# A two-layer hybrid trunk on one core: the scheduler orders the instructions by a simulated timeline

## The chip, the cores and the metric

The kernel runs on one core of one Trainium2 chip. A time is the device time of one execution of the whole program, in microseconds (us); less is better. Engines are written as in the profile: PE is TensorE (matmuls; PEld are its weight loads), DVE is VectorE, ACT is ScalarE, POOL is GpSimd, SP is SyncE, which issues nearly all DMAs. "L421" is line 421 of the kernel file.

## The reference

The reference is the trunk of a diffusion model: two layers over 256 latent tokens and 256 context tokens with 1024 channels, all in float32. Per layer:

```python
h = modulate(rmsnorm(x, norm1_g[l]), sh1, sc1)          # shifts and scales are silu(c) @ w_ada + b_ada
p = h @ w_in[l]                                         # GLU halves, q, k, v, gates
y_conv = conv_branch(p[..., :GLU_END], ...)             # GLU, depthwise conv of 31 taps, LayerNorm, silu, @ w_conv_out
y_attn = merge_heads(neighbourhood_attention(q, k, v, k_c, v_c, rpb)) @ w_na_out[l]
x = x + g1 * gated_merge(p[..., QKV_END:], y_conv, y_attn, w_out[l])
h2 = modulate(rmsnorm(x, norm2_g[l]), sh2, sc2)
x = x + g2 * conv_ffn(h2, w_up[l], ffn_dw[l], ffn_dw_b[l], w_down[l])   # FFN 2816, conv of width 3
```

Eight heads of 64 channels attend to a window of a 64-wide grid and to all context tokens. The context stream goes through the same weights, but its second layer needs only keys and values. A final RMSNorm ends it.

## The kernel before

Everything lies transposed: channels on the 128 partitions, tokens (256 latent, then 256 context) along the free axis, so a matmul has a 128x128 block of weights as stationary operand and 512 tokens (256 in the last layer) as moving one. float32 products are made of three fp32r products (L176 to L179): the weight and the activation are each split into a high and a low part.

```python
def mm3(ps, w, xh, xl, start, stop):
    pe.matmul(ps, w[0], xh, start=start, stop=False)     # L177
    pe.matmul(ps, w[0], xl, start=False, stop=False)     # L178
    pe.matmul(ps, w[1], xh, start=False, stop=stop)      # L179
```

Weights come in units of 128x1024 (512 KB) that SP fetches into one of four "raw" buffers (L155); ACT rounds a unit to its high part (`whi`, L158) and DVE subtracts to get the low part (`wlo`, L159). PSUM has four banks for `main`, two for `sc` (head scores), one for `pt` (transposes) and one for `po`.

The program is written as one row of weight groups. Other work is cut into steps by generators, and `slot()`, called within and behind each group, advances every generator that is open by one step. These side rows are:

- Attention of a layer. `product` (L417 to L421) makes the scores of two heads, each on its own 64 rows of the array, for 128 queries; `ctx` products are the same with 256 columns. `scores` (L437 to L445) adds the bias (DVE, L437), takes the maximum (DVE, L439), the exponential (ACT, L442), the reciprocal of the sum (DVE, L444) and multiplies (ACT, L445). `turn` transposes the probabilities on PE (L475, L480), ACT copies them (L476, L481), and `values` (L494) multiplies with V, each head on its own 64 columns of the array; L500 and L501 split the output. Queries and keys get their rotary part and their split on DVE at L740 to L747.

```python
for n, (a, b) in enumerate(((0, 0), (0, 1), (1, 0))):
    for o, r in zip(out, HALF):
        pe.matmul(o, q[r, a, c], k[r, b, d], start=n == 0, stop=n == 2)      # L421
```

- The depthwise convolution of 31 taps per channel tile, one DVE instruction per tap (L566, L568), at a fixed number of taps a step; the LayerNorm behind it.
- The adaLN products of later parts: on PE at the start and in the middle (L200, four groups of 32 columns; ACT copies the rows at L217, PE transposes them at L224), on DVE as dot products (L260) otherwise.
- The norms. The residual is added at L877, squares are summed (ACT L307, DVE L311), PE sums them over the channels with a column of ones (L325, tile `pt`), DVE scales (`red`, L333), POOL takes the power -1/2 (`rs`, L335), PE spreads it over the partitions (L340, tile `po`), and `modulated` makes h: DVE L354, ACT's high part L355, DVE's low part L356. In the FFN of layer 1 and behind the output projection of layer 0 this lies beside matmuls of other tiles.

No engine order is written out by hand, save a few edges (`tc.issue_after`). The functions above emit instructions in program order; the tile framework's scheduler then builds, from their dependences, one queue for each engine, with the semaphores between them, and hands out the slots of the pools in that order. [...]

## Time and profile before

| | |
|---|---|
| time, three runs | 1138.9, 1140.42, 1144.16 us (median 1140.42) |
| the profiled execution | time 1141.42 us, span 1139.6 us, mean granted PE clock 0.996 |
| instructions in the span | 17741 |
| HBM read | 187.57 MB, 166 GB/s over the span |
| stages (by the timeline) | start to 62 us; attention of layer 0, 75 to 205; output side and norm 2, 205 to 402; FFN, 402 to 725; layer 1's attention, 800 to 880; its FFN from 955; tail from 1130 |

The span runs from the first to the last instruction; the profiled execution's time has 1.8 us around it. A row of the timeline gives start, duration, engine, line, operation, what is written from what, shape and count (instructions of one kind in a row are joined); a square bracket gives idle time before it and who ended it. Matmuls overlap, so the step from one start to the next tells more than a duration.

### The profile page before, as it was taken

To read this page: it belongs to the slowest core of one execution; us is meant where nothing else is said; L and a number is where in the kernel's file an instruction comes from. 1 tells how busy PE (TensorE), PEld (TensorE's weight loads), DVE (VectorE), ACT (ScalarE), POOL (GpSimd) and SP (SyncE) were. 2 spreads that over 40 slices of the span, in tenths; PEclk is the share of its full clock that TensorE was granted. 3 is DMA by queue.
4 is the path that set the end of the run, shared out by engine and by line. 5 is a ranking of instruction groups with operands and counts; after the bars stand their busy time and mean duration, and the time that the engine had idled before them with its cause. 6 is when DMAs were issued, how large, how long until landed. Compare 5 with 4: busy or idle time off the path is not lost.

```text
span 1139.6 us, 17741 instructions
## 1 busy us (share of the span) xinstructions
PE 1123.0 (99%) x6854; PEld 962.8 (84%) x6854; DVE 916.4 (80%) x1620; ACT 567.9 (50%) x930; POOL 17.3 (2%) x25
## 2 busy tenths in 40 slices
PE   9999999999999999999999999999999999999997
PEld 7677777787779978888888888988889999999996
DVE  4689999937598698888888555789997889988773
ACT  4357667424334444343434222544678577666541
POOL 0000000000000000000000000010000000000000
PEclk9999999999999999999999999999999999999999
DMA  8832312644645255554557666565434574666781
GB/s 323 304 101 72 102 49 91 208 143 133 198 150 168 74 154 161 163 170 137 177 147 236 210 195 193 183 194 156 134 114 153 162 236 148 215 186 185 224 258 56
DMA packets 54949, 189.78 MB, mean 167 GB/s; under 512 B 6352, under 2 KB 6352, under 8 KB 54864
## 3 DMA queue, kind: packets, MB, share of 16 engines
q1 hardware_dynamic: 54576, 188.60, 52.8%
q8 instruction: 54, 0.88, 0.3%
q14 instruction: 31, 0.25, 0.1%
q10 hardware_dynamic: 288, 0.04, 0.0%
HBM read 187.57 MB, written 1.05 MB: 166 GB/s over the span
## 4 chain that ended last, share of the span: by engine, by line
PE 73%; issue 17%; DVE 5%; DMA 2%; ACT 2%; POOL 0%; POOLq 0%; DVEq 0%; ACTq 0%; SPq 0%
PE main L177 20%; PE main L179 20%; PE main L178 20%; PE main L621 4%; PE po L494 2%; PE sc L421 2%; DMA raw<-in_wall 2%; DVE wlo L159 1%; PE sc L127 1%; ACT whi L158 1%; PE pt L475 1%; DVE t L260 1%; PE po L200 1%; PE sc L179 1%; PE main L475 1%
## 5 line engine op out<-in xcount | busy, mean ns | idle before, releaser
L177 PE MATMUL main<-h,whi 128*128 128x256 f32 (+1 forms) x1328 | 449.1, 338 | 1.1 <-ACT h L871 0.5
L179 PE MATMUL main<-h,wlo 128*128 128x256 f32 (+1 forms) x1328 | 444.1, 335 | 0.9 <-DVE wlo L159 0.9
L178 PE MATMUL main<-h,whi 128*128 128x256 f32 (+1 forms) x1328 | 443.0, 334 | 1.0 <-DVE h L872 1.0
L158 ACT CAST whi<-raw 128x1024 fp32r<-128x1024 f32 (+1 forms) x244 | 252.3, 1038 | 285.4 <-PE main L178 136.5
L159 DVE TENSOR_TENSOR wlo<-raw,whi 128x1024 fp32r<-128x1024 f32 (+1 forms) x244 | 293.0, 1207 | 115.5 <-ACT whi L158 110.8
L177 PEld LDWEIGHTS main<-h,whi 128*128 128x128 f32 x1328 | 249.6, 188 | 33.4 <-issue 5.7
L179 PEld LDWEIGHTS main<-h,wlo 128*128 128x128 f32 x1328 | 249.9, 188 | 29.7 <-DVE wlo L159 1.7
L178 PEld LDWEIGHTS main<-h,whi 128*128 128x128 f32 x1328 | 250.1, 188 | 29.2 <-DVE h L872 1.5
L568 DVE SCALAR_TENSOR_TENSOR cb<-u,par,cb 128x512 f32<-128x512 f32 (+1 forms) x240 | 140.1, 616 | 1.2
L260 DVE CUSTOM_DVE_ANT_0 t<-raw,sb,par 128x1024 bf16<-128x1024 f32 x100 | 126.8, 1278 | 2.3 <-DMA raw<-in_wada 2.3
L177 PE MATMUL main<-fh,whi 128*128 128x256 f32 (+1 forms) x386 | 123.0, 319 | 0.0
L178 PE MATMUL main<-fl,whi 128*128 128x256 f32 (+1 forms) x386 | 122.9, 318 | 0.0
L179 PE MATMUL main<-fh,wlo 128*128 128x256 f32 (+1 forms) x386 | 122.9, 318 | 0.0
L940 ACT ACTIVATE t<-main,par 128x512 f32<-128x512 f32 (+1 forms) x82 | 50.8, 669 | 62.6 <-PE main L179 62.5
L178 PEld LDWEIGHTS main<-fl,whi 128*128 128x128 f32 x386 | 72.7, 188 | 5.6
L179 PEld LDWEIGHTS main<-fh,wlo 128*128 128x128 f32 x386 | 72.7, 188 | 5.6
L177 PEld LDWEIGHTS main<-fh,whi 128*128 128x128 f32 x386 | 72.7, 188 | 5.5
L941 DVE SCALAR_TENSOR_TENSOR t<-main,par,t 128x510 f32<-128x510 f32 (+1 forms) x82 | 47.7, 615 | 13.6 <-ACT t L940 13.3
L944 DVE SCALAR_TENSOR_TENSOR t<-main,par,t 128x510 f32<-128x510 f32 (+1 forms) x82 | 46.8, 610 | 0.0
L355 ACT ACTIVATE h<-t,mod 128x256 fp32r<-128x256 f32 x56 | 25.0, 501 | 34.7 <-DVE t L354 34.7
L966 ACT CAST fh<-t 128x256 fp32r<-128x256 f32 (+1 forms) x43 | 22.0, 511 | 37.9 <-DVE t L956 37.3
L621 PE MATMUL main<-whi,h 128*128 128x512 f32 x128 | 40.6, 402 | 0.0
(178 smaller groups left out, 1194.0 us busy)
## 6 DMA issues: line engine op xcount, KB each, us to landing
raw<-in_wall SPq DMA_DIRECT2D x239, 512.0 KB, 4.2
raw<-in_wada SPq DMA_DIRECT2D x88, 512.0 KB, 4.3
bias<-in_bias_t SPq DMA_DIRECT2D x16, 256.0 KB, 3.9
row<-in_wada SPq DMA_DIRECT2D x8, 512.0 KB, 4.9
sb<-in_crow SPq DMA_DIRECT2D x5, 512.0 KB, 5.2
x<-in_xt SPq DMA_DIRECT2D x8, 256.0 KB, 4.2
raw<-in_wall SPq DMA_DIRECT2D x8, 256.0 KB, 7.3
out<-t SPq DMA_DIRECT2D x4, 256.0 KB, 2.6
```

The lines of the kernel that those rows point to most:

```text
L158: act.copy(hi[:, c], r[:, c])
L159: dve.tensor_tensor(lo[:, c], r[:, c], hi[:, c].bitcast(F32), ALU.subtract)
L177: pe.matmul(ps, w[0], xh, start=start, stop=False)
L178: pe.matmul(ps, w[0], xl, start=False, stop=False)
L179: pe.matmul(ps, w[1], xh, start=False, stop=stop)
L260: dve.tensor_tensor_reduce(tmp().bitcast(BF16), r, v, 1.0, pr(l, BADA + n, 1), ALU.mult, ALU.add, mods[l][:, n, s : s + 1])
L355: high = act.activation(hi[:, c], y[:, c], AF.Identity, bias=b)
L568: dve.scalar_tensor_tensor(cb[j], src, w, cb[j], ALU.mult, ALU.add)
L621: pe.matmul(pv[t], h1[n == 1][k][:, c], w[n == 2][:, b], start=k + n == 0, stop=k == KD - 1 and n == 2)
L940: act.activation(c, pv_, AF.Identity, bias=pr(l, FDB + t, 1), scale=w[1])
L941: dve.scalar_tensor_tensor(c[:, :, 1:], pv_[:, :, : S - 1], w[0], c[:, :, 1:], ALU.mult, ALU.add)
L944: dve.scalar_tensor_tensor(c[:, :, : S - 1], pv_[:, :, 1:], w[2], c[:, :, : S - 1], ALU.mult, ALU.add)
```

## The change

One argument of the context in which the program is built. Without it the scheduler takes, for each engine, what is ready from a list; with it the scheduler plays the program on a simulated timeline of the engines and orders every engine's queue by that.

```diff
@@ -1168,7 +1168,7 @@
     out = nc.dram_tensor("out_0", (KD // 2, P, 2 * S), F32, kind="ExternalOutput").ap()
-    with tile.TileContext(nc) as tc:
+    with tile.TileContext(nc, schedule_with_timeline_sim=True) as tc:
         trunk(tc, *args, out)
```

The instructions are the same, but for the loads of ACT's function table, of which there are 15 in place of 17. Each engine's queue has another order, and 654 of 2105 tiles another slot of their pool. At three places that the prediction speaks of, the listings of the two programs read as follows (line, operation, tile written <- tiles read, shape; x3 is three in a row).

PE in layer 0's attention, scores of the first head pair for the second half of the queries (`sc_862` and `sc_863` are the two heads'). Before:

```order
L178 MATMUL main_827<-h_205,whi_829 128x512
L179 MATMUL main_827<-h_197,wlo_830 128x512
L421 MATMUL sc_862<-qk_761,qk_715 128x512
L421 MATMUL sc_863<-qk_761,qk_715 128x512
L421 MATMUL sc_862<-qk_761,qk_715 128x512
L421 MATMUL sc_863<-qk_761,qk_715 128x512
L421 MATMUL sc_862<-qk_761,qk_715 128x512
L421 MATMUL sc_863<-qk_761,qk_715 128x512
L177 MATMUL main_895<-h_190,whi_897 128x512
L178 MATMUL main_895<-h_198,whi_897 128x512
```

and with the change:

```order
L178 MATMUL main_895<-h_205,whi_897 128x512
L179 MATMUL main_895<-h_197,wlo_898 128x512
L421 MATMUL sc_862<-qk_761,qk_715 128x512 x3
L421 MATMUL sc_863<-qk_761,qk_715 128x512 x3
L475 MATMUL pt_944<-ident,pp_812 128x128 x4
L475 MATMUL main_951<-ident,pp_821 128x128 x4
L177 MATMUL main_989<-h_190,whi_991 128x512
L178 MATMUL main_989<-h_198,whi_991 128x512
L179 MATMUL main_989<-h_190,wlo_992 128x512
```

The six matmuls of the two heads no longer alternate, three of one head come before three of the other, and transposes (L475) follow where a weight group did.

DVE in layer 0's attention, softmax of the last head pair (`sc_1725` and `sc_1726` are scores, `mx` maxima, `ri` reciprocals, `cb` the convolution's sums). Before:

```order
L568 SCALAR_TENSOR_TENSOR cb_2_208<-u_0_219,par,cb_2_208 128x512
L566 TENSOR_SCALAR cb_3_209<-u_1_220,par 128x512
L437 TENSOR_TENSOR sc_1725<-sc_1725,bias_1525 128x256
L437 TENSOR_TENSOR sc_1726<-sc_1726,bias_1525 128x256
L439 TENSOR_REDUCE mx_1748<-sc_1725 128x1
L439 TENSOR_REDUCE mx_1757<-sc_1726 128x1
L568 SCALAR_TENSOR_TENSOR cb_2_208<-u_0_219,par,cb_2_208 128x512
L444 RECIPROCAL ri_1753<-sm_1751 128x1
L159 TENSOR_TENSOR wlo_1982<-raw_1980,whi_1981 128x1024
L444 RECIPROCAL ri_1762<-sm_1760 128x1
```

and with the change:

```order
L501 TENSOR_TENSOR ol_2_216<-po_1670,oh_2_212 128x512
L437 TENSOR_TENSOR sc_1725<-sc_1725,bias_1525 128x256
L437 TENSOR_TENSOR sc_1726<-sc_1726,bias_1525 128x256
L568 SCALAR_TENSOR_TENSOR cb_2_208<-u_0_219,par,cb_2_208 128x512
L568 SCALAR_TENSOR_TENSOR cb_3_209<-u_1_220,par,cb_3_209 128x512
L439 TENSOR_REDUCE mx_1748<-sc_1725 128x1
L439 TENSOR_REDUCE mx_1757<-sc_1726 128x1
L568 SCALAR_TENSOR_TENSOR cb_3_209<-u_1_220,par,cb_3_209 128x512
L159 TENSOR_TENSOR wlo_2114<-raw_2112,whi_2113 128x1024
L568 SCALAR_TENSOR_TENSOR cb_3_209<-u_1_220,par,cb_3_209 128x512
L444 RECIPROCAL ri_1753<-sm_1751 128x1
L444 RECIPROCAL ri_1762<-sm_1760 128x1
```

The taps of `cb_2` up to there and many of `cb_3` now stand ahead of these rows; of the ones shown, four taps of `cb_2` and `cb_3` and a split (`wlo_2114`, which stood further behind) lie within the softmax.

PE at the norm behind layer 0's output projection (`pt_3325` the sums of the latent stream, `po_3361` the spread rsqrt, `h_2548` on the first tile of the normalised h's high part). Before, with the twelve rows between as a line of dots:

```order
L178 MATMUL main_3312<-h_2562,whi_3155 128x256
L325 MATMUL pt_3325<-one,ss_2983 128x1 x2
L179 MATMUL main_3312<-h_2554,wlo_3156 128x256
L177 MATMUL main_3312<-h_2555,whi_3155 128x256
L178 MATMUL main_3312<-h_2563,whi_3155 128x256
...
L179 MATMUL main_3348<-h_2551,wlo_3162 128x256
L340 MATMUL po_3361<-ident,rs_3330 128x128 x2
L177 MATMUL main_3348<-h_2552,whi_3161 128x256
```

and with the change:

```order
L177 MATMUL main_3450<-h_2555,whi_3173 128x256
L178 MATMUL main_3450<-h_2563,whi_3173 128x256
L179 MATMUL main_3450<-h_2555,wlo_3174 128x256
L325 MATMUL pt_3325<-one,ss_2983 128x1 x2
L340 MATMUL po_3361<-ident,rs_3330 128x128 x2
L177 MATMUL sc_3508<-h_2548,whi_3485 128x256
L177 MATMUL sc_3509<-h_2548,whi_3491 128x256
L177 MATMUL main_3510<-h_2548,whi_3497 128x256
```

The sums and the transposes have moved behind the last group of the output projection (`main_3450`), and the first matmuls that read the normalised h (`h_2548`, on `sc_3508` and others) come right behind them.

## The prediction

> **What bounds the kernel now.** I read the page's engine row first, then the list of waits, then busy time by stretch, then the timeline at the places that the change touches.
>
> From the page of before:
>
> ```profile
> PE 1123.0 (99%) x6854; PEld 962.8 (84%) x6854; DVE 916.4 (80%) x1620; ACT 567.9 (50%) x930; POOL 17.3 (2%) x25
> ```
>
> TensorE is busy for 1123.0 of 1139.6 us. The kernel is a row of matmuls, and a new order can win only the gaps in that row. The list of waits of PE (engine, line, who is waited for: us in total, times, longest) says how much that is:
>
> ```profile
> PE sc L127 <- POOL ident masks.py:199: 1.8, 1, 1.8
> PE pt L325 <- DVE ss L311: 1.8, 2, 1.4
> PE main L179 <- DVE wlo L159: 1.8, 3, 0.9
> PE po L340 <- POOL rs L335: 1.6, 2, 1.1
> PE main L178 <- DVE h L872: 1.0, 1, 1.0
> PE pt L325 <- DVE t L303: 0.7, 1, 0.7
> PE main L177 <- ACT h L871: 0.5, 1, 0.5
> PE main L177 <- DVE t L944: 0.5, 1, 0.5
> PE sc L179 <- DVE wlo L159: 0.3, 1, 0.3
> ```
>
> They sum to 10.0 us. The first (1.8, the start) and the tail's chain (0.7 for L303, 1.1 of L335) have no other work to put in front of them, so at most 6.4 us can be won by order. Busy time by stretch (stretch, length, then PE, PEld, DVE, ACT, POOL with counts; PEclk; DMA share; GB/s) shows who is next:
>
> ```profile
> 75.00:205.00 130.00, 130.00 (x692) 97.54 (x691) 128.12 (x238) 89.11 (x175) 2.96 (x2) 1.00 0.27 84
> 800.00:880.00 80.00, 80.00 (x588) 68.50 (x588) 76.77 (x175) 60.73 (x120) 2.44 (x2) 1.00 0.44 132
> ```
>
> In the attention of layer 0 (75 to 205 us) VectorE is busy 128.12 of 130 us, 99%, beside a full PE: 1.9 us are free. In layer 1's it is 96%. Whatever puts VectorE's rows in a worse order there has almost no room to be hidden.
>
> The profiled execution's span is 1139.6 us and its time 1141.42, so 1.8 us lie around the span; its time is 1.0 above the median of the three runs (1140.42). The sum below starts from 1141.4.
>
> **A. Broken pairs of 64-row matmuls (L421).** A head pair's scores are six matmuls on 64 rows each, three per head. Before, the heads alternate in the queue; the timeline (start, duration, engine, line) shows what that gives:
>
> ```profile
> 78.64 0.39 PE L178 MATMUL main<-h,whi 128*128 128x512 f32 x1
> 78.87 0.40 PE L179 MATMUL main<-h,wlo 128*128 128x512 f32 x1
> 79.19 0.96 PE L421 MATMUL sc<-qk,qk 64*128 64x512 f32 x6
> 80.09 0.50 PE L177 MATMUL main<-h,whi 128*128 128x512 f32 x1
> 80.42 0.39 PE L178 MATMUL main<-h,whi 128*128 128x512 f32 x1
> ...
> 186.35 0.98 PE L421 MATMUL sc<-qk,qk 64*128 64x256 f32 x12
> 187.25 0.66 PE L475 MATMUL pt<-ident,pp 128*128 128x128 f32 x4
> ```
>
> A full-height 512 matmul takes a step of 0.23 us (78.64 to 78.87). The six of L421 take 79.19 to 80.09, 0.90 us: three steps of 0.23 and 0.2, not six. So two matmuls on different row halves run together when they are neighbours. The twelve of 256 columns take 0.90 too: six steps of 0.12 and 0.2. In the new order many steps have three of one head and then three of the other (the order shown under the change: x3, then x3). Only the last of the first head and the first of the second are neighbours, so three slots become five. Counting slots so over the whole listing, the 512 form goes from 48 to 71 and the 256 form from 24 to 39: 23 x 0.233 + 15 x 0.118 = 5.4 + 1.8 = 7.1 us, of which layer 0 has 8 and 15 (3.6 us) and layer 1 has 15 and 0 (3.5 us). No row of before shows an unpaired 64-row matmul. The bounds are nothing (the half that waits is taken by something else) and a full step each; I take the step, since the 64-row row is nearest and nothing else in the listing fits the free half.
>
> [...]
>
> **B and C. Column halves and visits.** The values (L494) pair two column halves:
>
> ```profile
> 100.92 1.95 PE L494 MATMUL po<-pT,V 128*64 128x256 f32 x16
> 102.80 0.50 PE L177 MATMUL main<-h,whi 128*128 128x512 f32 x1
> ```
>
> The trace records each of these instructions twice: sixteen records are eight instructions in four paired slots, 1.88 / 4 = 0.47 us. The new order has 46 slots for 40: 4 more in layer 0, 2 in layer 1, 1.9 and 0.9 us. Each change between a full array and a part of it costs 0.1 to 0.2 us: 78.87 to 79.19 is 0.32 for a step of 0.23, the six of L421 have 0.2 over, 80.09 to 80.42 is 0.33. The listing has 114 such changes for 88, so 26 x 0.15 = 3.9: 2.0 in layer 0, 1.1 in layer 1, 0.8 at the start (L200, 3 visits more). A to C make 7.5 us in layer 0 and 5.5 in layer 1.
>
> **D. VectorE in layer 0's attention.** The taps of the depthwise convolution (L568) come ahead of the softmax of the last head pair (the listing with sc_1725 under the change is one piece). In all, 33 instructions that stood behind the reciprocal ri_1753 now stand ahead of it: 29 taps, 3 splits (L159), one L501.
>
> ```profile
> 174.87 0.15 DVE L444 RECIPROCAL ri<-sm 128x1 f32<-128x1 f32 x1
> 184.66 3.38 DVE L568 SCALAR_TENSOR_TENSOR cb<-u,par,cb 128x512 f32<-128x512 f32 x5
> 189.82 1.22 DVE L159 TENSOR_TENSOR wlo<-raw,whi 128x1024 fp32r<-128x1024 f32 x1
> 175.07 0.74 ACT L445 ACTIVATE pp<-pp,ri 128x512 f32<-128x512 f32 x1
> ```
>
> A tap is 3.38 / 5 = 0.68 us, a split 1.22: 29 x 0.68 + 3 x 1.22 + 0.7 = 24 us. The reciprocal moves from 174.87 to about 199 and, after ScalarE's multiply (0.74), the transposes of L475 (pt_1885) can start at 199.8. PE had them at 187.25, and in its new order, by its own steps, gets there 12 matmuls sooner, at 186.4. So PE is 13.4 us early, less the 1.9 us that VectorE had free: 11.5. A to C in layer 0 (7.5) lie inside these 11.5, because they are PE time that passes while VectorE works; the rest, 4, is standing still. Bounds: 7.5 (VectorE finds more room than its busy share shows) and 16 (its lateness adds to some of A to C after that point). I take 11.5, as the rows stand.
>
> **E. Norm chains end to end.** At two places (before: 359.56 and 944.19 us) the new order has the column sums (L325), the transposes (L340) and the first matmul of the normalised h in a row, with nothing between. At the tail this chain is unhidden already, and its links are quoted first; then those of the first place before:
>
> ```profile
> 1131.01 0.61 PE L325 MATMUL pt<-one,t 128*128 128x1 f32 x4 [0.70 <-DVE t L303]
> 1131.73 0.16 DVE L333 TENSOR_SCALAR red<-pt 128x2 f32<-128x2 f32 x1 [0.77 <-PE pt L325]
> 1132.72 0.43 PE L340 MATMUL po<-ident,rs 128*128 128x128 f32 x2 [1.10 <-POOL rs L335]
> 1133.19 2.73 DVE L1061 TENSOR_TENSOR t<-x,po 128x256 f32<-128x256 f32 x8 [1.30 <-PE po L340]
> ...
> 359.56 0.61 PE L325 MATMUL pt<-one,ss 128*128 128x1 f32 x4
> 362.01 0.38 PE L340 MATMUL po<-ident,rs 128*128 128x128 f32 x2
> 363.23 1.65 DVE L354 SCALAR_TENSOR_TENSOR t<-x,gain,po 128x256 f32<-128x256 f32 x4
> ...
> 16.86 0.91 ACT L355 ACTIVATE h<-t,mod 128x256 fp32r<-128x256 f32 x2 [1.51 <-DVE t L354]
> ```
>
> L325 to L340 is 1.71 us (1131.01 to 1132.72), L340 to VectorE's product 0.47, one product 1.65 / 4 = 0.41, ScalarE's high part 0.91 / 2 = 0.46: 3.05 us, of which some 0.6 is PE's own work that was there before. Left bare: 2.45. Before, 2.4 us of matmuls stood between the first two links (359.56 to 362.01) and more behind. VectorE's queue adds to it: all four L354 (1.65) at the first place and five (2.06) at the second come ahead of the first low part (L356), for which L178 waits, 0.7 and 1.35 more; a split (L159) between the links adds 0.3 at the first. 3.4 + 3.8 = 7.2 us. Bounds: 4.9 (bare chains alone) and 9.
>
> **F. The start.** Two transposes of L224 now stand right behind the L200 whose rows ScalarE must copy first. Row pattern before:
>
> ```profile
> 14.33 0.71 PE L127 MATMUL sc<-ident 128*128 128x128 f32 x4
> 14.47 0.37 ACT L217 COPY t<-po 128x256 f32<-128x256 f32 x1 [3.01 <-PE po L200]
> 14.89 0.45 PE L224 MATMUL pt<-ident,t 128*128 128x128 f32 x2
> ...
> 10.98 0.33 SPq L145 DMA_DIRECT2D raw<-in_wada  x1
> ```
>
> PE had other work from 14.33 and L224 could start at 14.89: 0.6 bare, twice 1.2; the same at the first L494, which now stands right behind the transposes whose copy it reads, 0.7; and a weight unit of the adaLN products whose transfer is issued two places later on SP's queue, at 0.33 us an issue, 0.7. Sum 2.6, with the 0.8 of C 3.4; bounds 1 and 5.
>
> **G. Old waits gone.** Of the 6.4 us, the listing puts matmuls ahead of all but one split (0.9): 5 us won, bounds 3.5 and 6.4. The two FFN stretches (402 to 725, 960 to 1128) keep PE's order: nothing.
>
> **Sum.** 11.5 + 5.5 + 7.2 + 3.4 - 5 = 22.6; 1141.4 + 22.6 = 1164.0, less 1.0 for the median: 1163. With all low ends (7.5, 3.5, 4.9, 1, -6.4) 1151; with all high ends (16, 7, 9, 5, -3.5) 1174.
>
> **Rivals.** 1. *PE starts what is ready behind a blocked matmul.* Then the pairs come together again and the work behind each late operand fills its wait: A, B, D, E and most of F go, C's 3.9 stays, G's 5 is won: 1140, no change or faster. It decides from about 13 us (some 57 matmuls of 0.23 us) of reach; with a reach of six matmuls only A goes, and the time is still about 1160, since D then fills up. Against it: before, PE stood 1.4 us at an L325 with ready matmuls behind it. Chance 0.06.
>
> 2. *The clock.* Before, PE's few idle moments cost no clock except at the start:
>
> ```profile
> 15.00:16.00 1.00, 1.00 (x7) 0.90 (x7) 0.50 (x3) 0.36 (x1) 0.14 (x1) 0.59 1.07 422
> 16.00:17.00 1.00, 1.00 (x7) 1.00 (x6) 0.65 (x2) 0.14 (x1) 0.00 (x0) 0.50 1.00 393
> ```
>
> Here the granted clock is 0.59 and 0.50 after a thin stretch, for some 3.4 us. If each of D's and E's three stalls did that, half of 3.4 is lost each time, 5 us in all: 1168. Against it: stalls of 1.4 us later in the trace left it at 1.00. Chance 0.12. [...]
>
> 3. *Buffers come free later.* Tiles take other slots of their pools in the new order, so a weight unit's transfer may start later than I see. The page has its landing time:
>
> ```profile
> raw<-in_wall SPq DMA_DIRECT2D x239, 512.0 KB, 4.2
> ```
>
> Three units late by a whole landing would add 12.6: 1176. For it: four raw buffers only; against: SP's order hardly moves. Chance 0.16.
>
> That the change does nothing is excluded by the listings.
>
> **Chances.** The forecast has 0.66, the rivals the rest. A difference under 0.5% (5.7 us) could not be told from no change here: faster 0.03 and same 0.04 (together rival 1 and a rest), slower 0.93. The range goes from the low ends, 1150, to rival 3, 1177.
>
> **What the profile after would show.** A: L421 rows of x3 with 0.23 each rather than six in 0.9. D: a wait of PE at L475 on ScalarE's L445, or at L421 on VectorE's L747, of about 4 us, around 190 to 200 us. E: waits L325, L340 and L177/L178 of 2 to 4 us at about 385 and 975. Wrong would be: L421 still paired, VectorE's waits hidden, or PE waits of more than 2 us in an FFN.

## The result: 1189.6 us, and where the time went

The changed kernel takes 1189.62 us (median; 1187.14 to 1190.22), the kernel before beside it 1139.66: a ratio of 1.0424 [1.0397, 1.0451]. It is slower, as forecast, but by 50 us where 22.6 were forecast. The profiled execution's span is 1188.4 us (before 1139.6) and its mean granted PE clock 0.980 (before 0.996).

The profile after, first the page's engine row:

```profile
PE 1150.3 (97%) x6854; PEld 979.9 (82%) x6854; DVE 911.5 (77%) x1620; ACT 564.5 (47%) x928; POOL 14.9 (1%) x25
```

PE has the same 6854 instructions and is busy 27.3 us longer. The other 21.5 of the 48.8 us by which the span grew are idle time. So there are two losses of nearly one size: PE waits more, and it takes longer for the same work. The list of waits of PE of the changed kernel (engine, line, who is waited for: us in total, times, longest) gives the first:

```profile
PE sc L421 <- ACT pp L442: 6.6, 4, 3.2
PE main L177 <- ACT whi L158: 3.9, 3, 2.6
PE pt L475 <- ACT pp L445: 3.3, 4, 1.3
PE po L340 <- POOL rs L335: 3.2, 3, 1.1
PE main L475 <- ACT pp L445: 2.4, 3, 1.3
...
PE sc L177 <- ACT h L355: 2.2, 1, 2.2
```

The whole list sums to 31.4 us, where before's summed to 10.0. Three of the first five are links of the softmax: scores (L421) wait until an exponential (L442) has freed their bank, and transposes (L475) wait for the multiplied probabilities (L445). The old waits of that list on `ss` and on `wlo` are gone.

Busy time by stretch of the changed kernel (stretch, length, then PE, PEld, DVE, ACT, POOL with counts; PEclk; DMA share; GB/s) gives a part of the second loss:

```profile
165.00:170.70 5.70, 3.72 (x18) 2.21 (x17) 5.18 (x11) 3.81 (x7) 1.70 (x1) 1.00 0.22 76
170.70:174.10 3.40, 3.40 (x10) 2.63 (x9) 3.40 (x8) 1.65 (x4) 0.00 (x0) 0.50 0.08 29
204.80:211.70 6.90, 6.79 (x21) 5.37 (x22) 6.05 (x15) 5.38 (x13) 0.00 (x0) 0.51 0.27 76
392.60:399.40 6.80, 5.84 (x25) 5.55 (x26) 6.80 (x19) 4.11 (x10) 0.00 (x0) 0.50 0.22 80
843.10:850.00 6.90, 5.08 (x17) 3.97 (x18) 6.90 (x20) 4.07 (x9) 0.00 (x0) 0.51 0.41 115
996.70:1003.60 6.90, 6.00 (x26) 5.71 (x27) 6.90 (x19) 4.44 (x12) 0.00 (x0) 0.51 0.00 0
```

From 165 to 170.7 PE works 3.72 of 5.7 us at full clock (two waits, of 0.68 and 1.30 us, lie there); then for 3.4 us the granted clock is 0.50. The rows below it are four more such stretches, twice as long. With one at about 106 and one at 969 us there are seven between the start and the tail, 41 us in all. PE is busy for most of each, and the step from one 512-column matmul to the next is 0.43 us there (209.34 to 209.77 us) against 0.23 at full clock (212.02 to 212.25). Before had none between 19 us and its tail.

The same matmuls matched between the two traces give the losses by place: the time at which a matmul starts after, less the time at which it starts before, read at the edges of the stages. The split is worked out from the same steps: a wait is the time in which PE is idle, the half clock's part is put at half of PE's busy time in a half-clock stretch (by the steps of 0.43 and 0.23 us it is 0.46), and what is left over is PE's own instructions, or matmuls that changed places across an edge. Each part is good to about 1 us.

| stage (times of before) | change, us | of it waits | of it half clock |
|---|---|---|---|
| start, to 70 | +3.6 | 3.3 | -1.7 |
| attention of layer 0, 70 to 235 | +20.5 | 5.8 | 8.0 |
| 235 to 355 | -3.4 | -2.5 | 0 |
| first norm place, 355 to 385 | +5.3 | 3.1 | 2.9 |
| 385 to 420 | -1.5 | -1.1 | 0 |
| FFN of layer 0, 420 to 725 | 0.0 | 0 | 0 |
| 725 to 780 | -1.6 | -0.9 | 0 |
| attention of layer 1, 780 to 905 | +14.3 | 7.6 | 2.5 |
| 905 to 940 | +5.6 | 3.7 | 1.5 |
| second norm place, 940 to 960 | +4.3 | 1.3 | 3.0 |
| 960 to the end | +1.9 | 1.2 | 0.1 |

That sums to 49.0 us for 48.8 in the spans: about 21 us of waits, 16 of clock, and 11 of PE's own instructions, of which L421 has 4.9 and L494 2.9. (The clock's -1.7 at the start is a half-clock stretch that before has there and the changed kernel has not.)

Three places in the changed kernel's timeline (start, duration, engine, line, operation; idle time before and who ended it in square brackets). At 205 us, in layer 0's attention:

```profile
202.64 1.04 ACT L158 CAST whi<-raw 128x1024 fp32r<-128x1024 f32 x1 [4.45 <-PE main L178]
203.59 0.58 ACT L605 COPY g<-main 128x512 f32<-128x512 f32 x1
204.07 0.69 ACT L442 ACTIVATE pp<-sc,mx 128x512 f32<-128x512 f32 x1
...
204.91 1.64 PE L421 MATMUL sc<-qk,qk 64*128 64x512 f32 x4 [2.06 <-ACT pp L442]
```

Scores wait for a bank that an exponential must free. The exponential stands behind a cast on ScalarE, and the cast itself stood idle 4.45 us for a buffer that PE had to free. Then, at the first norm place:

```profile
389.16 0.50 PE L325 MATMUL pt<-one,ss 128*128 128x1 f32 x4
390.74 0.43 PE L340 MATMUL po<-ident,rs 128*128 128x128 f32 x2 [1.08 <-POOL rs L335]
393.42 0.80 PE L177 MATMUL sc<-h,whi 128*128 128x256 f32 x2 [2.25 <-ACT h L355]
```

This is the bare chain of step E. And at 965 us, a place of which the prediction says nothing:

```profile
964.78 1.28 ACT L244 ACT_TABLE_LOAD   x1 [6.68 <-DMA sb<-in_crow]
966.07 1.06 ACT L244 ACTIVATE sb<-sb 128x1024 f32<-128x1024 f32 x1
967.03 1.03 ACT L158 CAST whi<-raw 128x1024 fp32r<-128x1024 f32 x1
968.11 0.39 PE L177 MATMUL main<-h,whi 128*128 128x256 f32 x1 [2.56 <-ACT whi L158]
```

The silu of the conditioning row (L244), which waits for a transfer, was put ahead of a weight unit's cast on ScalarE; ScalarE stands 6.68 us, and PE 2.56 behind it.

### The profile page after: what moved, and what is told of

Same layout as the page of the kernel before. It is cut to its first block, busy times and chain, and to the rows that moved or that the text cites. A ratio compares the mean times of both kernels' runs of the same rounds, so it can differ in the third digit from the quotient of the medians.

```text
span 1188.4 us, 17896 instructions
## 1 busy us (share of the span) xinstructions
PE 1150.3 (97%) x6854; PEld 979.9 (82%) x6854; DVE 911.5 (77%) x1620; ACT 564.5 (47%) x928; POOL 14.9 (1%) x25
## 4 chain that ended last, share of the span: by engine, by line
PE 73%; issue 17%; DVE 6%; ACT 2%; DMA 2%; POOL 0%; SPq 0%; POOLq 0%; DVEq 0%; ACTq 0%
PE main L177 20%; PE main L179 20%; PE main L178 19%; PE main L621 4%; PE po L494 2%; PE sc L421 1%; DVE cb L568 1%; DVE wlo L159 1%; DMA sb<-in_crow 1%; PE sc L179 1%; PE sc L178 1%; PE sc L177 1%; ACT whi L158 1%; PE sc L127 1%; PE main L475 1%
## 5 line engine op out<-in xcount | busy, mean ns | idle before, releaser
L177 PE MATMUL main<-h,whi 128*128 128x256 f32 (+1 forms) x1328 | 450.9, 342 | 6.2 <-ACT whi L158 3.9
L158 ACT CAST whi<-raw 128x1024 fp32r<-128x1024 f32 (+1 forms) x244 | 252.6, 1038 | 391.4 <-PE main L178 261.4
L177 PEld LDWEIGHTS main<-h,whi 128*128 128x128 f32 x1328 | 253.2, 191 | 36.7 <-ACT whi L158 6.3
L178 PEld LDWEIGHTS main<-h,whi 128*128 128x128 f32 x1328 | 253.9, 191 | 31.0 <-issue 2.8
L179 PEld LDWEIGHTS main<-h,wlo 128*128 128x128 f32 x1328 | 253.6, 191 | 30.4 <-issue 2.5
L260 DVE CUSTOM_DVE_ANT_0 t<-raw,sb,par 128x1024 bf16<-128x1024 f32 x100 | 125.1, 1281 | 7.9 <-DMA raw<-in_wada 6.2
L177 PE MATMUL main<-fh,whi 128*128 128x256 f32 (+1 forms) x386 | 122.7, 319 | 0.0
L177 PEld LDWEIGHTS main<-fh,whi 128*128 128x128 f32 x386 | 72.6, 188 | 5.6
L877 DVE SCALAR_TENSOR_TENSOR x<-main,mod,x 128x256 f32<-128x256 f32 x48 | 22.1, 482 | 34.2 <-PE main L179 34.2
```

Of the source, the lines that this page charges most:

```text
L158: act.copy(hi[:, c], r[:, c])
L260: dve.tensor_tensor_reduce(tmp().bitcast(BF16), r, v, 1.0, pr(l, BADA + n, 1), ALU.mult, ALU.add, mods[l][:, n, s : s + 1])
```

## The experiments

Most of them are the kernel before with parts of the new queues. A helper lists an engine's instructions in a given order and adds an order edge, without a semaphore, from each to the next; the scheduler then has no choice:

```diff
+def pin(tc, nc, engine, spec):
+    ins = [i for i in nc.cur_bb.bb.instructions if i.engine == engine]
...
+    for a, b in zip(order, order[1:]):
+        tc.add_manual_dep(ins[b], ins[a].name, NO_SYNC)
```

With all five queues of the changed kernel listed so, the kernel before becomes the changed kernel, instruction for instruction. So any one stage, or one engine within it, can be given the new order while the rest keeps the old.

### Pairs apart: step A alone

Before's queues; in PE's alone, all score matmuls of one head come ahead of the other head's (24 groups).

```diff
-L421 sc_a, sc_b, sc_a, sc_b, sc_a, sc_b
+L421 sc_a, sc_a, sc_a, sc_b, sc_b, sc_b
```

> The kernel before, with every queue in its own order, but that PE takes all matmuls of one head of a pair (L421) before those of the other, in all 24 groups. Step A of the prediction: the 16 groups of 512 columns go from three slots to five (2 x 0.233 us each, 7.5 us) and the four double groups of 256 from six to eleven (5 x 0.118 us each, 2.4 us): 9.8 us more, about 1150 us. Rival: TensorE starts a matmul of the free row half although it stands behind others of the busy half; then nothing changes, 1140 us, and each group still takes 0.9 us in the trace.

Measured 1.0014 [0.9999, 1.0029]. Two pieces of its timeline on PE:

```profile
78.04 0.97 PE L421 MATMUL sc<-qk,qk 64*128 64x512 f32 x6
78.94 0.50 PE L177 MATMUL main<-h,whi 128*128 128x512 f32 x1
...
91.38 1.32 PE L421 MATMUL sc<-qk,qk 64*128 64x256 f32 x12
```

Six matmuls queued 3 + 3 still take 78.04 to 78.94 = 0.90 us, as when they alternated. The single records show the second head's first matmul, fourth in the queue, starting 0.01 us behind the first head's first. Only with twelve, queued 6 + 6, does it start later, with the third, and the twelve take about 1.25 us instead of 0.91: 4 x 0.34 = 1.4 us in all. So TensorE does pass matmuls in front that sit on the other row half, two of them here and three in the groups of twelve; as far as that, it doesn't take its queue in order. Step A's two slots for a row of 3 + 3 are refuted. In the changed kernel some pairs do run apart, for other reasons: the second head's bank is not free in time (6 x 256 columns alone at 102.56 us, the other six at 104.21 after a wait), or other matmuls stand between the two heads, as in these rows of the changed kernel:

```profile
899.13 0.96 PE L421 MATMUL sc<-qk,qk 64*128 64x512 f32 x3
900.03 0.65 PE L494 MATMUL po<-pT,V 128*64 128x256 f32 x2
900.60 0.96 PE L421 MATMUL sc<-qk,qk 64*128 64x512 f32 x3
```

Three matmuls alone take 0.90 us (899.13 to 900.03), as long as six that stand together.

### The norms alone, and filled

Before's queues with the new order at the two norm places only; then the same with idle matmuls that nothing reads, between the links of the chain:

```diff
+    pe.matmul(bank[:, 256:384], ident, ident, start=True, stop=True)   # 4 behind L325 and 8 or 5 behind L340
```

> The kernel before, but all engines take the changed kernel's order in two short stretches, 355 to 380 and 940 to 957 us, which hold the two norm chains that were laid end to end. The prediction (E alone, the clock untouched): 7.2 us more, less up to 2 us of old waits at these places, about 1146 us. Rival, the clock: each chain's waits are followed by 6.8 us at half the granted clock, which costs up to 3.4 us at each place: 12 to 14 us more, about 1153 us.

> As norms, with 24 idle matmuls on the identity in the two chains: five between the sums (L325) and the transposes (L340), nine and five behind L340, each writing columns that nothing reads. They lie inside the waits. The prediction's step E: no change against norms, or some tenths more where a filler outlasts the wait. The clock rival: PE's activity no longer falls, the two half-clock stretches are missing in the trace, and the time is 4 to 7 us below norms although the kernel does more.

> As norms_fill, with the idle matmuls all on the bank that L325 used (four ahead of L340, eight and five behind it), so that VectorE's reads of the other bank do not wait for them. Clock rival: no half-clock stretch at the two places, and 3 to 6 us less than norms (1149.96 us), 1144 to 1147 us. If the clock costs nothing there, no change against norms, 1150 us or more.

The norms alone: 1.0072 [1.0046, 1.0098], 1149.96 us. Its timeline on PE has the chains of step E, at the first and the second place:

```profile
368.32 0.43 PE L340 MATMUL po<-ident,rs 128*128 128x128 f32 x2 [1.08 <-POOL rs L335]
370.57 0.51 PE L177 MATMUL sc<-h,whi 128*128 128x256 f32 x2 [1.82 <-ACT h L355]
371.94 0.58 PE L178 MATMUL sc<-h,whi 128*128 128x256 f32 x1 [0.62 <-DVE h L356]
...
956.62 0.43 PE L340 MATMUL po<-ident,rs 128*128 128x128 f32 x2 [1.03 <-POOL rs L335]
958.17 0.68 PE L177 MATMUL main<-h,whi 128*128 128x256 f32 x2 [1.12 <-ACT h L355]
959.59 0.58 PE L178 MATMUL main<-h,whi 128*128 128x256 f32 x1 [0.74 <-DVE h L356]
```

The waits sum to 3.5 and 2.9 us. The first filled version gave 1.0093 [1.0066, 1.0119] and doesn't separate anything: its idle matmuls behind L340 wrote into the tile that VectorE was to read, the program's semaphore released VectorE only behind the last of them, and the chain from L325 to the first L177 grew from 3.8 to 5.5 and from 3.1 to 4.6 us. The second, with all of them on the bank of L325, gave 1.0051 [1.0034, 1.0069], 1148.51. Busy time by stretch, of the norms alone (columns as above; ahead of the half clock and in it, at both places):

```profile
365.00:371.00 6.00, 3.10 (x26) 2.77 (x25) 4.42 (x8) 5.55 (x9) 0.70 (x1) 1.00 0.60 175
371.20:378.10 6.90, 6.28 (x31) 6.16 (x30) 5.69 (x15) 2.92 (x8) 0.00 (x0) 0.51 0.18 66
954.00:958.30 4.30, 2.16 (x18) 1.83 (x17) 1.36 (x5) 1.33 (x6) 0.70 (x1) 1.00 0.26 103
958.30:965.20 6.90, 6.16 (x28) 5.87 (x29) 6.51 (x18) 4.44 (x12) 0.00 (x0) 0.51 0.00 1
```

and with idle matmuls (the second version):

```profile
368.50:374.60 6.10, 5.79 (x51) 5.65 (x49) 4.49 (x9) 5.65 (x9) 0.70 (x1) 1.00 0.61 181
374.60:381.50 6.90, 6.27 (x52) 5.89 (x51) 5.98 (x17) 3.05 (x8) 0.01 (x1) 1.00 0.17 63
954.00:958.40 4.40, 4.15 (x35) 3.88 (x35) 1.23 (x4) 1.20 (x6) 0.70 (x1) 1.00 0.22 88
958.40:965.30 6.90, 5.45 (x42) 5.04 (x42) 6.64 (x18) 4.44 (x11) 0.00 (x0) 1.00 0.00 1
```

PE is busy 5.79 us instead of 3.10 ahead of the place, and the clock stays at 1.00 behind it. With more work on PE the matched matmuls come 2.5 and 1.4 us earlier than in the norms alone. (The whole kernel gains less, 1.4 us between medians, and the intervals overlap; 0.9 us of the second gain is lost again by 1000 us, and the profiled execution of the filled kernel had a half-clock stretch of 6.8 us at the start, which that of the norms alone had not.) So the half clock follows from PE's thin stretch, and is a cost of its own beside the wait.

The traces say more closely when it comes. In each of the 18, the granted clock falls only at points that lie whole multiples of 3.41 us apart, so I count PE's work in windows of that length. Of the full-clock windows (without the first 20 and the last 12 us of a trace), the 39 in which PE was busy for under 1.55 us all had a half-clock window behind them; of 5782 with more than 2.3 us only one had, the first below, in which 12 of the 18 matmuls use 64 rows; and of the 57 between, 19 had. The windows ahead of three of the changed kernel's stretches:

```profile
102.38:105.80 3.42, 2.73 (x18) 1.96 (x16) 3.42 (x9) 3.36 (x8) 0.00 (x0) 1.00 0.02 8
167.29:170.70 3.41, 2.11 (x12) 1.46 (x13) 3.41 (x5) 1.96 (x4) 1.70 (x1) 1.00 0.37 127
201.40:204.83 3.43, 1.44 (x7) 0.83 (x5) 3.41 (x5) 2.19 (x5) 1.58 (x1) 1.00 0.00 0
```

By these counts the same wait can cost nothing or a whole stretch, by where it falls. PE was not idle in the windows ahead of the changed kernel's seven stretches: it was busy for 0.5 to 2.7 us in them, and its longest single wait is 3.2 us.

### The attentions alone, and the silu alone

```diff
-L421/L475/L494 and the rest of the stage, all five queues: order of before
+                                                        order of the changed kernel
```

> The kernel before, but all engines take the changed kernel's order in the two attentions, 70 to 235 and 780 to 905 us. The prediction: 11.5 + 5.5 = 17 us more, 1157 us. From the shift between the two traces at matched matmuls (3.6 to 24.1 us over layer 0's attention, 22.8 to 37.1 over layer 1's): 20.5 + 14.3 = 35 us more, 1175 us, if the stages add up. A time near 1157 would say that the loss comes from elsewhere in the program.

> The kernel before, but all engines take the changed kernel's order between 905 and 940 us, where ScalarE has the silu of a broadcast row (L244, fed by a DMA) ahead of the casts of two weight units (L158). The prediction counted nothing here: 1140 us. From the changed kernel's trace, where ScalarE waited 6.7 us for that DMA and PE 2.6 and 1.2 us for the casts, with 3.4 us of half clock behind it: 4 to 7 us more, 1144 to 1147 us.

Both attentions: 1.0294 [1.0271, 1.0317], and at matched matmuls +20.7 us in layer 0 and +15.2 in layer 1, nearly as in the changed kernel itself (20.5 and 14.3). The silu's stretch (905 to 940) alone: 1.0057 [1.0034, 1.0080], 1148.32 us, with PE's waits at L177 on L158 summing to 3.6 us, the longest 2.2. Stage by stage the loss stays where it arises: at no later place do these runs give back more than 0.8 us.

### One engine's order at a time

PE's queue alone as new in layer 0's attention; and the changed kernel with one engine's whole queue as before.

```diff
-pin(tc, nc, PE, BEFORE)
+pin(tc, nc, PE, NEW_IN_LAYER_0_ATTENTION)     # all other engines as before
```

> The kernel before, but PE alone takes the instructions of layer 0's attention (70 to 235 us) in the changed kernel's order; VectorE, ScalarE and SP keep the order of before. The prediction (A to C in layer 0, without VectorE's late rows): 7.5 us more, 1147 to 1148 us. If PE's own order makes the waits (steps of the attention that follow each other closer than the softmax takes): 15 us or more. If pairs cost nothing and VectorE's order made the rest: 2 to 4 us (column halves and visits alone), about 1143 us.

> The changed kernel (ordered by the simulated timeline), but PE's queue is held in the order of the kernel before; VectorE, ScalarE, POOL and SP get the orders that the simulated timeline finds beside it. If PE's order carries the loss: 1140 to 1150 us, no wait of PE above 2 us in the attentions. If VectorE's and ScalarE's orders carry it (the prediction's D): above 1160 us.

> The changed kernel, but VectorE's queue is held in the order of the kernel before; PE and the others get the orders that the simulated timeline finds beside it. If VectorE's order carries the attention's loss (the prediction's D): the two attentions come back to within 10 us of before, 1165 us or less. If PE's order does: 1180 us or more, since PE's steps are still put by the simulated timeline.

PE alone: 1.0243 [1.0212, 1.0275]. At matched matmuls the stage loses 27.3 us, more than all five queues together cost there (20.5). The first rows of its list of waits:

```profile
PE po L494 <- ACT pT L476: 4.6, 1, 4.6
PE pt L224 <- ACT t L217: 4.0, 1, 4.0
PE main L177 <- DVE u L584: 3.4, 1, 3.4
```

The changed kernel with PE as before: 1.0481 [1.0460, 1.0501]; with VectorE as before: 1.0547 [1.0528, 1.0566]. In both, layer 0's attention loses only 7 to 8 us instead of 20.5, and other places lose more (with PE as before 41 us have been lost by the end of layer 1's attention, for 37, and an L325 waits 6.3 us for its squares). The queues are one set: the order of one engine is only good or bad against the others'. No run gives VectorE or ScalarE alone the new order within a stage.

### VectorE's load taken away: step D

The changed kernel's five queues with every second tap of the convolution on 32 of the 256 tokens, which leaves that part of the convolution out.

```diff
-dve.scalar_tensor_tensor(cb[j], src, w, cb[j], ALU.mult, ALU.add)
+r = (S, 32)[t % 2]
+dve.scalar_tensor_tensor(cb[j][:, :, :r], src[:, :, :r], w, cb[j][:, :, :r], ALU.mult, ALU.add)
```

> The changed kernel's queues on all engines, but every second tap of the depthwise convolution (L568) works on 32 of the 256 tokens of a stream, which leaves that part of the convolution out. VectorE has some 60 x 0.5 us less to do in layer 0's attention and 60 x 0.3 us in layer 1's; the order of all queues is the same. If VectorE's late softmax rows hold PE: most of the attention's waits and their half-clock stretches go, 15 to 28 us less than the changed kernel, 1162 to 1175 us. Rival, PE's own order: its steps follow closer than scores, ScalarE's exponential and copy take, whatever VectorE does: under 8 us less, above 1181 us.

Measured 1.0392 [1.0365, 1.0419], 1186.76 us: about 3 us less than the changed kernel, with the same 6.6 us of waits at L421 on L442. Layer 0's attention, at matched matmuls, loses the same 20.5 us. VectorE's work ahead of the last softmax, on which step D put 11.5 us, is not what PE waits for.

### ScalarE's exponentials first

The changed kernel's queues, with 18 exponentials moved ahead of the casts and gate copies that stood in front of them on ScalarE; once alone, once with the short taps too.

```diff
-L158 CAST, L605 COPY, L442, L442
+L442, L442, L158 CAST, L605 COPY
```

> The changed kernel's queues, but on ScalarE the exponentials of the softmax (L442, L458) go ahead of a weight cast (L158) or gate copy (L605) that stands directly ahead of them or between the two of a pair; 18 exponentials move, by one or two places. If ScalarE's order holds PE (the cast waits for PE to free its buffer, PE waits for the exponential behind it to free a score bank): the waits at 103, 166 and 202 us go and with them at least one half-clock stretch, 5 to 12 us less than the changed kernel, 1177 to 1184 us. If VectorE's rows or PE's own steps hold it: within 3 us of the changed kernel, 1187 us or more.

> As exp_first, and with every second tap (L568) on 32 of 256 tokens, as in the run with short taps, which leaves that part of the convolution out. If VectorE and ScalarE hold PE by turns, so that one alone gives little: 10 to 20 us less than the changed kernel, 1169 to 1179 us. If PE's own order is too tight: no more than exp_first gives.

Measured 1.0459 [1.0439, 1.0479], 1193.32 us, and 1.0392 [1.0376, 1.0409], 1186.21: no gain, and one of 3 us that the short taps alone give too. Layer 0's attention loses 20.5 us again, and 18.4 with both. In place of the 2.06 us wait at 204.91 above:

```profile
202.95 1.63 PE L421 MATMUL sc<-qk,qk 64*128 64x512 f32 x6 [0.38 <-ACT pp L442]
207.37 1.05 PE L475 MATMUL pt<-ident,pp 128*128 128x128 f32 x4 [2.79 <-ACT pp L445]
```

The wait at the scores falls to 0.38 and the next link's becomes 2.79: the transposes then stand too soon. It isn't one late link: here PE comes to the next link before its operand is done.

### More room for the chain

The listings say how much room it has. Between a step's scores and its transposes PE has, in its own steps, 10.3 to 16.3 us of other matmuls before (median 14.0 in layer 0, 16.0 in layer 1), and 5.5 to 14.0 in the changed kernel (median 8.1 and 7.8). On the chip, from the start of a step's last score matmul to that of its first transpose, the distance in the changed kernel was 7.9 us or more in layer 0 and 7.1 or more in layer 1, with medians of 9.4 and 10.0. Where PE had to wait for the probabilities, they came 8.6 to 12.5 us behind the scores: so long bias, maximum, exponential, reciprocal and multiplication took there. So I had the step wait for two further steps before its transposes are emitted (L412), with the scheduler of the changed kernel, and as a control with that of before:

```diff
-            if self.soft and self.soft[0][0] >= 3:
+            if self.soft and self.soft[0][0] >= 5:
```

> The changed kernel, but the program emits the transposes of an attention step (turn) five slots behind its scores in place of three; the simulated timeline orders everything anew. PE's own work between a step's scores and its transposes grows in layer 0 from 5.5 to 14.0 us (median 8.1) to 9.7 to 12.4 us, in layer 1 it stays at 7.8 to 11.8. If that distance, against some 8 to 10 us that scores, softmax and multiply take on the chip, makes PE wait: layer 0's attention loses 10 us less than in the changed kernel, its waits and half-clock stretches mostly go, 1177 to 1182 us in all, and layer 1's loss stays. If it is something else in the order: 1187 us or more.

> The kernel before with the same edit, as a control: its distances are 10.3 us and more already, so the longer ones (15.9 us and more) should change nothing: 1138 to 1143 us.

Measured 1.0400 [1.0374, 1.0425] in the changed kernel and 1.0010 [0.9994, 1.0026] in the one before. The distance on the chip grew to a median of 12.6 us in layer 0 and 11.2 in layer 1. Layer 0's attention, at matched matmuls, loses 10.5 us instead of 20.5. Busy time over it, in the changed kernel:

```profile
70.00:235.00 165.00, 159.17 (x767) 116.46 (x765) 148.39 (x271) 90.62 (x179) 3.36 (x2) 0.95 0.26 80
```

and with two steps more:

```profile
70.00:230.00 160.00, 158.70 (x786) 116.18 (x786) 148.10 (x269) 91.72 (x181) 2.58 (x2) 1.00 0.28 86
```

PE idles 1.3 us there instead of 5.8, and the clock stays at 1.00. That bears out the chain's room as the cause of layer 0's waits and of the half clock behind them. The rest of that stage's loss is PE's own instructions, 9.2 us here and 6.7 in the changed kernel: 5.0 of the 9.2 are L421's, whose heads stand apart in more of the pairs, 2.3 L494's and 1.1 L200's. The scheduler made its plan anew for the whole program, though, so the room isn't all that changed, and the gain was lost elsewhere: 3.3 us of waiting at an L325 at 379 us and a half clock from 382.7 to 392.9. In layer 1 the loss to 905 us was 12.5 us instead of 14.3 (4.7 of waits for 7.6, no half clock, and 7.7 of own instructions for 4.1), and some 5 us more came right behind, where PE waited for the convolution's output (L840, L841, L864). With PE's old queue it was 16.1 us. So in layer 1 the cause isn't settled.

### The stages that gained

Three stages were quicker in the changed kernel, by 6.5 us in sum. (Of the last one's 1.6 us, up to 0.9 may be no gain of the order: of the runs with the old order there, four (the second filled version, both attentions, the silu alone, and PE alone) are 0.8 to 0.9 us quicker than the profiled execution of before, too, while the norms alone, the first filled version and the second version below are not.) Before's queues with the new order in those alone (235 to 355, 385 to 420, 720 to 775), and a second version without the part behind 330 us and the last stage:

```diff
-235 to 355, 385 to 420, 720 to 775: order of before
+                                    order of the changed kernel
```

> The kernel before, but all engines take the changed kernel's order in three stretches in which PE gained time between the two traces: 235 to 355, 385 to 420 and 720 to 775 us (shifts of -3.4, -1.5 and -1.6 us at matched matmuls). If the stages add up: 6 us less than before, 1133 to 1135 us. If the waits only move on to the next stage: 1140 us.

> As best, but with the changed kernel's order in 235 to 330 and 385 to 420 us alone: the stretch from 720 us is left out, behind which PE waited 2.5 us for an exponential, and the first ends before the dot products on VectorE that made PE wait 2.9 us at the norm. 4 to 6 us less than before, 1135 to 1137 us, if the gains of the two stretches stand; 1140 us if they are given back again.

Measured 1.0033 [1.0020, 1.0045] and 0.9990 [0.9975, 1.0004]. The first is up to 4.1 us ahead by 340 us, and then waits:

```profile
359.39 0.60 PE L325 MATMUL pt<-one,ss 128*128 128x1 f32 x4 [2.92 <-DVE ss L311]
```

PE is early, and the squares (L311) aren't, with dot products (L260) ahead of them on VectorE; a half clock follows (0.95 over 345 to 380 us). Nothing of the gain remains in either, and no version beats the kernel before.

## Why the prediction was right in its sign and wrong in its size

**A was mis-argued, and its size was near in layer 0 only.** 7.1 us were put on broken pairs, 3.6 in layer 0 and 3.5 in layer 1. The step, two slots more for a row of 3 + 3, is false: such a row costs nothing, and the groups of twelve cost 1.4 us in all (pairs apart). Rival 1, TensorE starting ready matmuls behind others, was right in kind, with the reach of a few matmuls at which, as its text says, only A goes. The wait in front of ready matmuls that the prediction held against it (1.4 us at an L325) was at matmuls on the full height and says nothing of the row halves. L421 still grew by 3.1 us in layer 0 and 1.8 in layer 1 outside the half clock, but by other pairs: two whose second head waited for its bank (1.0 us each, without the wait), one with L494 between the heads (0.9), three that stand 2 + 4 with other matmuls between (0.2 each), and the tails of waits. That the sum came near 3.6 in layer 0 is luck.

**B and C** came out near their size where they could be read: L494's rows grew by 2.9 us outside the half clock, for 2.8. By shape, in the changed kernel:

```profile
L494 PE MATMUL po<-pT,V 128*64 128x256 f32 x160 | 24.2, 392 | 1.1 <-ACT pT L476 1.1
```

(24.2 us busy, 3.9 above before's 20.3, with the half clock in it). Changes between full and part array weren't isolated.

**D failed in cause and size.** It had 11.5 us for layer 0's attention, 7.5 of it from A to C and 4 of standing still, behind VectorE's taps. The stage lost 20.5: 5.8 of waits, 8.0 of clock, 6.7 of longer instructions. The last are what A to C put at 7.5, and they came on top of the waits instead of lying inside VectorE's lateness. The waits are on the softmax's chain through both engines. Shorter taps leave them as they are (6.6 us at L421 over both layers, and the same 20.5 for the stage); two steps more between scores and transposes take most of them away, and the half clock with them. The predicted wait at 190 to 200 us, on L445 or L747, was at 202.9, on an exponential (L442), and of 2.06 us, not 4.

**Layer 1's attention** had 5.5 us, all from A to C, and lost 14.3: 4.1 of longer instructions, 7.6 of waits that the prediction didn't look for there, and 2.5 of clock. Why PE waits there is not settled.

**E was about right.** The chains alone wait 3.5 and 2.9 us, for 3.4 and 3.8. What is missing is some 3 us of clock at each place.

**F** was 3.4 us and measured 3.6, which is luck in part: the half clock at the start isn't the same in every execution (3.4 us in that of before, 6.8 in the second filled version's, none in the norms alone's), and kernels with the old order there were between 1.0 us ahead of the profiled execution of before (the norms alone) and 2.7 behind it (the second filled version) at 65 us. **G** was -5; the gaining stages sum to -6.5. The FFN stretches were to keep their time, and that of layer 0 does, to 0.0 us.

**The clock** was only a rival, with 5 us for three stalls, and counts about 18 over seven stretches. The argument against it, that stalls of 1.4 us left the clock at 1.00, was drawn from single stalls in a full row. The least filled window of before behind its start (325.8 to 329.2 us) still holds 2.0 us of PE's work. The changed kernel's stalls come two or three together or reach 2 us and leave 0.5 to 1.5 us in five of the seven windows (2.1 and 2.7 in the others), and then up to half of a stretch of 3.4 or 6.8 us is lost, 1.7 or 3.4 us (2.9 and 3.0 at the norm places), not 1.7 each time.

**Missed** was the silu at 905 to 940 (5.6 us): an instruction that waits for a transfer moved ahead of a cast on ScalarE. The prediction followed ScalarE's order at none of its places, only PE's, VectorE's and, at the start, SP's.

Place by place, measured less forecast: layer 0's attention 20.5 for 11.5 (+9.0), layer 1's 14.3 for 5.5 (+8.8), the norms 9.6 for 7.2 (+2.4), the silu 5.6 for nothing, the start 3.6 for 3.4 (+0.2), the gaining stages -6.5 for -5 (-1.5), the end 1.9 for nothing: 26.4 more than 22.6, the 49.0 of the table.

## What to carry to other kernels

Where one engine is 99% busy, an order by a simulated timeline is as good as its durations: compare the room that it leaves on that engine between the two ends of a chain (here 8 us of matmuls in the median) with what the chain takes on the chip (8.6 to 12.5 us where PE waited), link by link and on every engine that it crosses. Price a stall of TensorE with the clock that follows it: waits that left it busy for 0.9 and 1.5 us of a window of 3.41 us cost 2.9 and 3.0 us more at the two norm places here, and with idle matmuls on a bank that nobody waits for the clock stayed at 1.00 there, instead of 0.51 in the norms alone. An order of queues is one set: the stages that lost carried their losses over to the old order, and those that gained did not carry their gains.

## What the runs showed of the hardware

- A matmul on a free row half of the array started ahead of two queued ones on the other half (six queued 3 + 3, in 0.90 us) or three (twelve queued 6 + 6, in about 1.25 us instead of 0.91).
- The granted clock fell to 0.50 only at points whole multiples of 3.41 us apart, for 3.4, 6.8 or 10.2 us. Behind a full-clock window between such points in which PE was busy for under 1.55 us it always fell (39 of 39, in 18 traces); with more than 2.3 us once in 5782, and between the two 19 times in 57. With idle matmuls in the gaps (PE at 5.79 of 6.1 and 4.15 of 4.4 us instead of 3.10 of 6.0 and 2.16 of 4.3) it didn't fall.
